# Two staging tiles, builds in fp32, and projections that stage values and split keys in a ring of five

## The chip, the cores and the metric

The kernel runs on one core of a Trainium2 chip. The metric is the device time of one execution in microseconds. TensorE is the engine of the matmuls, VectorE (DVE in the rows), ScalarE (ACT) and GpSimd (POOL) work on SBUF tiles, and SyncE (SP) issues nearly all plain transfers, in order; GpSimd issues the indirect ones.

## The reference, cut to what matters

One layer for two requests, 1024 prompt tokens and 64 sample tokens with 512 tokens of cache:

```python
h = rmsnorm(x)
zq, zk, zv, zcq, zckv, zkr, zg = split(h @ w_in)
o_a = differential_attention(zq, zk, zv)       # 8 heads, chunk-causal, relative bias
o_b = latent_attention(zcq, zckv, zkr)         # 16 heads, compressed keys and values
x = x + (sig(zg0) * (o_a @ w_a) + sig(zg1) * (o_b @ w_b)) @ w_out
h2 = rmsnorm(x)                                # expert part ("PEER"):
idx, g = two_stage_top16(h2 @ w_q, keys)       # 8 heads x 16 experts of 16384 per token
act = gelu(einsum("td,thkd->thk", h2, u[idx])) # 128 rows of u per token
x = x + einsum("thk,thkd->td", g * act, v[idx])
y = rmsnorm(x)
```

Outputs are y, the new keys and values and the new latents. All is fp32.

## The kernel before, in words

The 1088 tokens are nine tiles of 128 rows (the ninth has the 64 sample rows). Three groups of three tiles (`GROUPS`) go one after the other through projections, both attentions, output projection and expert scores. Group 0 splits its operands into two parts and uses three matmuls for one; groups 1 and 2 use plain fp32 matmuls. Then two passes over all of `peer_v` (`PASSES`: tiles 0 to 2, then 3 to 6) multiply a dense 128 x 16384 matrix of expert weights per tile with `peer_v`, in 16 chunks of 8 x 128 experts.

Beside this runs the expert part as background jobs, written as generators that `pump` advances while the main work is emitted: `route_job` (top-16, on VectorE), `dots_job`, `build_job`, and for tiles 8 and 7, which have no dense matrix, `vgather_job`. The job of a tile in a group's place runs in the next group; those of the last group run in the passes. The order that the chip gets is not quite the order of emission: a planner orders each engine's instructions with its own costs and the tiles' dependences, so a change of a tile's size or ring gives a new order everywhere. Each engine works through its list in order.

- **Dots (lines 338 to 365).** For each of the 128 experts of a row, `gather` (327) fetches one row of `peer_u` per token, 512 KB for a tile, with an indirect transfer from GpSimd into a buffer, and VectorE multiplies and sums it in place against h2 (line 358). There are four buffers `gb`, and in groups 1 and 2 three more, `gm`, in a pool `more` that opens when group 0 has given back its memory; three gathers of seven use `gm`. In the passes only `gb` exists. `vgather_job` uses the same `gather` on `peer_v` (line 453).
- **Builds (lines 367 to 426).** The dense matrix of a tile comes from its 128 indices and weights per token. The pair of indices of all experts of a token becomes two one-hot matrices, `oh1` and `oh2` (lines 402 and 403, 8 tokens at a time, a "step"; 16 steps per tile, 7 tiles, 112 steps). `oh2` is scaled by the weight, and a matmul over the 128 experts gives the token's 128 x 128 block. To keep fp32 weights in bf16 matmuls the weight is split into three bf16 parts (`a3`): three scaled copies `w3` (line 408 on ScalarE for part 0, eight instructions; line 411 on VectorE for parts 1 and 2) and three matmuls per token (line 418). ScalarE copies the result to `stage` (line 424), an 8 KB-per-partition tile that exists once; two steps fill it and one store writes it to `Ad` in memory. Of tile 6 (`TR`) the first `RC` = 9 chunks go into the resident tile `Ares` instead (line 422), and only the others to `Ad`; the passes load the rest as `araw`.
- **Projections.** `tmajor` makes 128 x 256 blocks. Keys go to `kt` (line 700, ring "P" of `PB` = 5 tiles), are transposed and split into `khl` (in the two-deep ring "Q") and stored to `kTd`. Values go through `vt` (line 720, the two-deep ring `z1`, which others use as well) and are stored to the output block by block.

Of the kernel before, what the change touches and what calls it, by code (L numbers as in the profile page):

```python
# [10 lines left out]
F32 = mybir.dt.float32  # L11
F32R = mybir.dt.float32r
BF16 = mybir.dt.bfloat16
I32 = mybir.dt.int32
U32 = mybir.dt.uint32
AF = mybir.ActivationFunctionType
ALU = mybir.AluOpType
# [3 lines left out]
D = 1024  # L21
# [16 lines left out]
GN = 384  # L38
# [2 lines left out]
NGB = 4  # L41
PB = 5
NB = 8
RC = 9
NWHOLE = 8
TR = 6
RATE_R2 = 0.41
# [12 lines left out]
def hybrid_tile(ctx: ExitStack, tc: tile.TileContext, A):  # L60
    nc = tc.nc
    V, S, G, PE, SP = nc.vector, nc.scalar, nc.gpsimd, nc.tensor, nc.sync

    def ld(out, in_):
        if out.dtype == F32R:
            out = out.bitcast(F32)
        if in_.dtype == F32R:
            in_ = in_.bitcast(F32)
        return SP.dma_start(out, in_)
# [34 lines left out]
    bp = ctx.enter_context(tc.tile_pool(name="bp", bufs=1))  # L104
# [10 lines left out]
    gturn = [0]  # L115
# [7 lines left out]
    def ptile(name, shape=(128, 1024), dt=F32):  # L123
        return att.tile(list(shape), dt, name=name, tag="P", bufs=PB)
# [10 lines left out]
    def z1(name):  # L135
        return sm.tile([128, 256], F32, name=name, tag="z1", bufs=2)
# [4 lines left out]
    def out_rows(name, t):  # L141
        return A[name + "_p"][t * 128:(t + 1) * 128] if t < 8 else A[name + "_s"]
# [183 lines left out]

    def gather(src, idx):
        gturn[0] += 1
        if cur["more"] and gturn[0] % 7 % 2:
            gb = cur["more"].tile([128, D], F32, name="gm", tag="gm")  # L330
        else:
            gb = cur["gp"].tile([128, D], F32, name="gb", tag="gb")
        G.indirect_dma_start(out=gb, out_offset=None, in_=src, in_offset=bass.IndirectOffsetOnAxis(ap=idx, axis=0))  # L333
        return gb
# [32 lines left out]
    def build_job(t):  # L367
        if t == TR:
            drain("r")
        src = bp.tile([128, 3, 128], F32, name="bsrc", tag="oh1")  # L370
        ld(src[:, 0, :], wgtd[t])
        ld(src[:, 1:3, :], efd[t])
        p = cur["ps"].tile([128, 512], F32, name="mm")
        pv = p.rearrange("p (a n) -> p a n", n=128)
        for i in range(3):
            PE.transpose(pv[:, i, :], src[:, i, :], ident)
        ixT = bp.tile([128, 2, 128], BF16, name="ixT")
        S.copy(ixT, pv[:, 1:3, :])
        aT = bp.tile([128, 128], F32, name="aT")
        S.copy(aT, pv[:, 0, :])  # L380
        a3 = bp.tile([128, 3, 128], BF16, name="a3")
        a3f = bp.tile([128, 128], F32, name="a3f")
        for i in range(3):
            V.tensor_copy(a3[:, i], aT)
            if i == 0:
                V.tensor_copy(a3f, a3[:, 0])
            if i < 2:
                V.tensor_tensor(aT, aT, a3[:, i], op=ALU.subtract)
        yield
        shp = [128, 4, 128, 2]  # L390
        iv = iota2[:, None, :, :].to_broadcast(shp)

        def over(row, tt):
            return row[:, tt:tt + 8].rearrange("p (g x) -> p g x", x=2)[:, :, None, :].to_broadcast(shp)

        n = RC if t == TR else 0
        for t0 in range(0, 128, 16):
            stage = bp.tile([128, 16, 4, 8, 4], F32, name="stage", tag="stage")
            for tt in range(t0, t0 + 16, 8):
                oh1 = bp.tile(shp, BF16, name="oh1", tag="oh1")  # L400
                oh2 = bp.tile(shp, BF16, name="oh2")
                V.tensor_tensor(oh1, iv, over(ixT[:, 1], tt), op=ALU.is_equal)  # L402
                V.tensor_tensor(oh2, iv, over(ixT[:, 0], tt), op=ALU.is_equal)  # L403
                w3 = bp.tile([128, 3] + shp[1:], BF16, name="w3")
                for i in range(3):
                    if i == 0:
                        for x in range(8):
                            S.activation(w3[:, 0, x // 2, :, x % 2], oh2[:, x // 2, :, x % 2], AF.Copy,  # L408
                                         scale=a3f[:, tt + x:tt + x + 1])
                    else:  # L410
                        V.tensor_tensor(w3[:, i], oh2, over(a3[:, i], tt), op=ALU.mult)
                for q in range(2):
                    p = cur["ps"].tile([128, 512], F32, name="mm")
                    pv = p.rearrange("p (a n) -> p a n", n=128)
                    for j in range(4):
                        x = 4 * q + j
                        for i in range(3):
                            PE.matmul(pv[:, j, :], lhsT=oh1[:, x // 2, :, x % 2], rhs=w3[:, i, x // 2, :, x % 2],  # L418
                                      start=i == 0, stop=i == 2)
                    pc = p.rearrange("p (t c i) -> p c i t", t=4, i=8)  # L420
                    if n:
                        S.copy(cur["Ares"][:, :, (tt + 4 * q) // 4], pc[:, :n])
                    if n < 16:
                        S.copy(stage[:, n:, (tt - t0) // 4 + q], pc[:, n:])
                    yield
            ld(Ad[t, :, n:, t0 // 4:t0 // 4 + 4], stage[:, n:])
# [149 lines left out]
    for g, tiles in enumerate(GROUPS):  # L576
# [117 lines left out]
        for j in range(4):  # L694
            w = wchunk(A["w_in"][2 + j])
            kt = ptile("kt", (128, 3, 256))
            for ti, t in enumerate(tiles):
                nr = tr(t)
                p = tmajor(hT, w, t)
                S.copy(kt[:nr, ti], p[:nr, :256])  # L700
                ld(out_rows("k", t)[:, j * 256:(j + 1) * 256], kt[:nr, ti])
            for hh in range(2):
                khl = att.tile([128, 2, GN], F32R, name="khl", tag="Q")
                pt = tpt()
                for ti, t in enumerate(tiles):
                    nr, l = tr(t), loc[t]
                    PE.transpose(pt[:, l:l + nr], kt[:nr, ti, hh * 128:hh * 128 + 128], ident[:nr, :nr])
                split(pt[:, :NH], khl[:, 0, :NH], khl[:, 1, :NH])
                dst = kTd[2 * j + hh]
                for i in range(2):  # L710
                    for l, tok, n in runs:
                        ld(bass.AP(tensor=dst.tensor, offset=dst.offset + 64 * i * T + tok,
                                   ap=[[(64 if i else 192) * T, 2], [T, 64], [1, n]]), khl[:, i, l:l + n])
        for j in range(4):
            w = wchunk(A["w_in"][6 + j])
            for t in tiles:
                nr = tr(t)
                p = tmajor(hT, w, t)
                vt = z1("vt")
                S.copy(vt[:nr], p[:nr, :256])  # L720
                ld(out_rows("v", t)[:, j * 256:(j + 1) * 256], vt[:nr])
        for j in range(8):
            w = wchunk(A["w_in"][14 + j])
            for hh in range(2):
# [613 lines left out]
```

## Time and profile before

| | |
|---|---|
| three runs | 4512.42, 4510.65, 4497.69 us; median 4510.65 |
| the profiled execution | 4499.18 us, its span 4497.4 us |
| TensorE, VectorE, ScalarE, GpSimd busy | 86%, 71%, 36%, 43% of the span |
| granted TensorE clock, mean | 0.892 of full speed |
| bytes moved | 1183 MB, 263 GB/s; 671 MB of it by the gathers |

The span counts from the first to the last instruction. Busy shares are means over stretches with different limits, so each stretch is read by itself. In a table of stretches the columns are the stretch, its length, the busy time of each engine (with its number of instructions), the granted clock of TensorE, the share of time that the DMA engines were in use, and GB/s. A row of waits says which engine sat idle before which instruction, and what ended that idle time.

### The profile page before, as it was taken

The numbers are of one execution on the slowest core, as the hardware profiler recorded it, in microseconds if no ns is written. First come the engines' busy times: TensorE is split into PE (matmuls) and PEld (weight loads), VectorE is DVE, ScalarE is ACT, GpSimd is POOL, SyncE is SP. The second block draws the span as 40 slices with busy tenths as digits, with TensorE's granted clock in tenths as the row PEclk, the third lists the DMA queues.
The fourth block names the chain that finished last, engine by engine and source line by source line (L and its number), as shares of the span: only waits on it lengthen the run. The fifth ranks groups of instructions, "written<-read, shape, count | busy, mean of one in ns | idle before, by whom it ended". The sixth has DMA issues, their size and how long they took to land.

```text
span 4497.4 us, 55226 instructions
## 1 busy us (share of the span) xinstructions
PE 3847.6 (86%) x18633; PEld 2898.2 (64%) x18633; DVE 3203.9 (71%) x7136; ACT 1603.3 (36%) x3656; POOL 1942.8 (43%) x1353
## 2 busy tenths in 40 slices
PE   6998988898788798887868877889999969999991
PEld 6977887556565565655546666654457858888881
DVE  4043457977788767797786777659847987777776
ACT  3344622025455513322454455133113532232320
POOL 3412241554456441143444656513434445545455
PEclk9967999987898898998778888989999979999995
DMA  5421244996777785697776767988868999989987
GB/s 176 168 96 56 67 170 169 352 350 231 267 263 269 272 320 216 226 329 290 245 248 239 256 239 253 351 291 311 320 246 317 349 328 332 351 312 352 321 314 260
DMA packets 467587, 1183.10 MB, mean 263 GB/s; under 512 B 45352, under 2 KB 218888, under 8 KB 452584
## 3 DMA queue, kind: packets, MB, share of 16 engines
q0 software_dynamic: 184320, 671.17, 41.4%
q1 hardware_dynamic: 282984, 508.41, 32.3%
q8 instruction: 147, 2.41, 0.2%
q14 instruction: 136, 1.11, 0.1%
HBM read 1074.60 MB, written 104.56 MB: 262 GB/s over the span
## 4 chain that ended last, share of the span: by engine, by line
PE 42%; DMA 13%; DVE 13%; issue 5%; ACT 4%; POOL 2%; SPq 0%; another core or an unknown queue 0%; ACTq 0%; POOLq 0%; DVEq 0%
PE acc_ps L1221 16%; PE mm L167 9%; PE acc_ps L1206 5%; DMA Ad<-stage 4%; DMA gb<-in_peer_v,beidx 3%; DVE gb L358 3%; DMA gb<-in_peer_u,beidx 2%; PE mm L418 2%; DVE gm L358 2%; POOL gb L333 2%; PE mm L827 2%; PE sc L795 1%; PE mm L952 1%; PE sc L793 1%; ACT w L408 1%
## 5 line engine op out<-in xcount | busy, mean ns | idle before, releaser
L333 POOL DMA_INDIRECT gb<-in_peer_u,beidx x758 | 1028.2, 1356 | 1364.7 <-DVE gb L358 811.1
L358 DVE SCALAR_TENSOR_TENSOR gb<-gb,h2r 128x1024 f32<-128x1024 f32 x758 | 918.3, 1220 | 174.4 <-DMA gb<-in_peer_u,beidx 157.9
L333 POOL DMA_INDIRECT gm<-in_peer_u,beidx x330 | 429.9, 1303 | 501.4 <-DVE gm L358 274.6
L1221 PE MATMUL acc_ps<-vhi,ahi 128*128 128x512 f32 x1408 | 439.9, 395 | 23.4 <-ACT ahi L1214 23.4
L1221 PE MATMUL acc_ps<-vhi,alo 128*128 128x512 f32 x1408 | 444.1, 396 | 3.0 <-DVE alo L1215 3.0
L1221 PE MATMUL acc_ps<-vlo,ahi 128*128 128x512 f32 x1408 | 441.0, 395 | 0.0
L358 DVE SCALAR_TENSOR_TENSOR gm<-gm,h2r 128x1024 f32<-128x1024 f32 x330 | 402.1, 1218 | 24.0 <-DMA gm<-in_peer_u,beidx 21.4
L333 POOL DMA_INDIRECT gb<-in_peer_v,beidx x192 | 268.0, 1396 | 229.7 <-DVE gacc L453 150.1
L167 PE MATMUL mm<-h,wraw 128*128 128x384 f32 (+1 forms) x1024 | 325.5, 479 | 20.4 <-ACT qd L739 10.4
L1206 PE MATMUL acc_ps<-vw,aw 128*128 128x512 f32 x768 | 335.0, 596 | 1.4 <-ACT aw L1202 1.4
L418 PE MATMUL mm<-w,oh 128*128 128x128 bf16 x2688 | 231.0, 237 | 111.5 <-DVE oh L402 50.5
L1221 PEld LDWEIGHTS acc_ps<-vhi,ahi 128*128 128x128 f32 x1408 | 265.6, 189 | 85.5 <-ACT ahi L1214 23.6
L453 DVE SCALAR_TENSOR_TENSOR gacc<-gb,vwgt,gacc 128x1024 f32<-128x1024 f32 x192 | 246.2, 1282 | 93.3 <-DMA gb<-in_peer_v,beidx 88.1
L1221 PEld LDWEIGHTS acc_ps<-vhi,alo 128*128 128x128 f32 x1408 | 265.0, 189 | 63.9 <-DVE alo L1215 3.7
L1221 PEld LDWEIGHTS acc_ps<-vlo,ahi 128*128 128x128 f32 x1408 | 265.5, 189 | 60.2 <-DVE vlo L1192 0.2
L408 ACT ACTIVATE w<-oh,a3f 128x128 bf16<-128x128 bf16 x896 | 280.8, 429 | 54.0 <-DVE oh L403 24.3
L179 POOL TENSOR_TENSOR wlo<-wraw,whi 128x2048 fp32r<-128x2048 f32 (+1 forms) x42 | 186.8, 4447 | 260.6 <-ACT whi L178 255.0
L418 PEld LDWEIGHTS <-oh 128*128 128x128 bf16 x2688 | 191.9, 106 | 160.6 <-issue 73.2
L167 PEld LDWEIGHTS mm<-h,wraw 128*128 128x128 f32 x1024 | 201.0, 199 | 133.8 <-issue 11.4
L167 PE MATMUL mm<-wraw,h 128*128 128x256 f32 (+1 forms) x960 | 235.6, 402 | 37.7 <-ACT vt L720 27.8
L1206 PEld LDWEIGHTS acc_ps<-vw,aw 128*128 128x128 f32 x768 | 145.5, 191 | 179.1 <-issue 175.6
L1214 ACT CAST ahi<-araw 128x1024 fp32r<-128x1024 f32 x79 | 82.8, 1049 | 474.4 <-PE acc_ps L1221 395.7
(384 smaller groups left out, 7574.2 us busy)
## 6 DMA issues: line engine op xcount, KB each, us to landing
vraw<-in_peer_v SPq DMA_DIRECT2D x192, 512.0 KB
wraw<-in_w_in SPq DMA_DIRECT2D x66, 1024.0 KB
araw<-Ad SPq DMA_DIRECT2D x103, 512.0 KB
Ad<-stage SPq DMA_DIRECT2D x48, 1024.0 KB
vw<-in_peer_v SPq DMA_DIRECT2D x64, 512.0 KB
wraw<-in_w_a SPq DMA_DIRECT2D x12, 1024.0 KB
wraw<-in_w_b SPq DMA_DIRECT2D x12, 1024.0 KB
wraw<-in_w_out SPq DMA_DIRECT2D x12, 1024.0 KB
```

What stands on the lines that cost most here:

```text
L167: PE.matmul(out, lhsT=L[0], rhs=R[0], start=start, stop=stop)
L179: G.tensor_tensor(lo[:, :n], raw[:, :n], hi[:, :n].bitcast(F32), op=ALU.subtract)
L333: G.indirect_dma_start(out=gb, out_offset=None, in_=src, in_offset=bass.IndirectOffsetOnAxis(ap=idx, axis=0))
L358: behind(V.scalar_tensor_tensor(gb, gb, 1.0, h2, op0=ALU.mult, op1=ALU.mult, accum_out=act[:, k:k + 1]))
L408: S.activation(w3[:, 0, x // 2, :, x % 2], oh2[:, x // 2, :, x % 2], AF.Copy, scale=a3f[:, tt + x:tt + x + 1])
L418: PE.matmul(pv[:, j, :], lhsT=oh1[:, x // 2, :, x % 2], rhs=w3[:, i, x // 2, :, x % 2], start=i == 0, stop=i == 2)
L453: behind(V.scalar_tensor_tensor(acc, gb, wgt[:, k:k + 1], acc, op0=ALU.mult, op1=ALU.add))
L793: PE.matmul(ps[:nq, a:b], lhsT=Q[:, c, qc:qc + nq], rhs=K[:, c, a - o:b - o], start=True, stop=False)
L827: PE.matmul(po[:nq, :128], lhsT=PT[:kw, b, :nq], rhs=Vt[:kw, b, :], start=b == 0, stop=b == nb - 1)
L1206: PE.matmul(pst[t][:, ds], lhsT=rv[:, i, :], rhs=vb[i][:, ds], start=c == 0 and i == 0, stop=False)
L1214: S.copy(av, rv)
L1221: PE.matmul(pst[t][:, ds], lhsT=L[:, i, :], rhs=R[:, ds], start=c == (0 if ip else NWHOLE and -1) and i == 0 and L is ahi and R is vb[i][0 ...
```

## The change

- `stage` becomes two tiles: the even ones stay in the pool `bp`, the odd ones come from the pool `more` in groups 1 and 2 and from `p2` in the passes.
- To make room, `gm` has one buffer instead of three, used by one gather of five, and `RC` is 7 instead of 9.
- A build's step has no split: `oh1` is copied to fp32 (`of`, ScalarE), `oh2` is multiplied by the fp32 weight (`w`, VectorE), and there is one fp32 matmul per token. `a3`, `a3f` and `w3` go.
- `khl` and `vt` are taken from the ring "P"; one `vt` holds the blocks of the group's three tiles.

```diff
-RC = 9
+RC = 7
...
-        if cur["more"] and gturn[0] % 7 % 2:
-            gb = cur["more"].tile([128, D], F32, name="gm", tag="gm")
+        if cur["more"] and gturn[0] % 5 == 1:
+            gb = cur["more"].tile([128, D], F32, name="gm", tag="gm", bufs=1)
...
-        a3 = bp.tile([128, 3, 128], BF16, name="a3")
-        a3f = bp.tile([128, 128], F32, name="a3f")
-        for i in range(3):
-            V.tensor_copy(a3[:, i], aT)
-            if i == 0:
-                V.tensor_copy(a3f, a3[:, 0])
-            if i < 2:
-                V.tensor_tensor(aT, aT, a3[:, i], op=ALU.subtract)
...
-            stage = bp.tile([128, 16, 4, 8, 4], F32, name="stage", tag="stage")
+            sp = (cur["more"] or cur["p2"]) if t0 % 32 else bp
+            stage = sp.tile([128, 16, 4, 8, 4], F32, name="stage", tag="stage", bufs=1)
...
-                w3 = bp.tile([128, 3] + shp[1:], BF16, name="w3")
-                for i in range(3):
-                    if i == 0:
-                        for x in range(8):
-                            S.activation(w3[:, 0, x // 2, :, x % 2], oh2[:, x // 2, :, x % 2], AF.Copy,
-                                         scale=a3f[:, tt + x:tt + x + 1])
-                    else:
-                        V.tensor_tensor(w3[:, i], oh2, over(a3[:, i], tt), op=ALU.mult)
+                of = bp.tile(shp, F32, name="of")
+                S.copy(of, oh1)
+                w = bp.tile(shp, F32, name="w")
+                V.tensor_tensor(w, oh2, over(aT, tt), op=ALU.mult)
...
-                        for i in range(3):
-                            PE.matmul(pv[:, j, :], lhsT=oh1[:, x // 2, :, x % 2], rhs=w3[:, i, x // 2, :, x % 2],
-                                      start=i == 0, stop=i == 2)
+                        PE.matmul(pv[:, j, :], lhsT=of[:, x // 2, :, x % 2], rhs=w[:, x // 2, :, x % 2],
+                                  start=True, stop=True)
...
-                khl = att.tile([128, 2, GN], F32R, name="khl", tag="Q")
+                khl = ptile("khl", (128, 2, GN), F32R)
...
-            for t in tiles:
+            vt = ptile("vt", (128, 3, 256))
+            for ti, t in enumerate(tiles):
                 nr = tr(t)
                 p = tmajor(hT, w, t)
-                vt = z1("vt")
-                S.copy(vt[:nr], p[:nr, :256])
-                ld(out_rows("v", t)[:, j * 256:(j + 1) * 256], vt[:nr])
+                S.copy(vt[:nr, ti], p[:nr, :256])
+                ld(out_rows("v", t)[:, j * 256:(j + 1) * 256], vt[:nr, ti])
```

## Rows read from the trace of the kernel before

**Rows 1.** The table of stretches: groups 1 and 2, attention, long pass, tail.

```profile
700.00:2975.00 2275.00, 1864.19 (x9375) 1360.30 (x9375) 1749.33 (x4235) 866.43 (x2267) 1024.46 (x768) 0.86 0.77 272
2045.00:2365.00 320.00, 231.41 (x1043) 156.97 (x1042) 243.99 (x453) 146.66 (x379) 126.03 (x92) 0.77 0.73 251
2420.00:2820.00 400.00, 324.44 (x2106) 259.35 (x2106) 304.08 (x512) 204.30 (x543) 233.75 (x151) 0.85 0.71 240
3690.00:4400.00 710.00, 709.46 (x3063) 575.95 (x3061) 552.29 (x610) 193.29 (x188) 386.90 (x274) 1.00 0.90 330
4400.00:4497.00 97.00, 0.00 (x0) 0.00 (x0) 66.44 (x103) 4.59 (x8) 49.20 (x39) 0.52 0.75 255
```

**Rows 2.** The chain that ended last, shares of the span by line (last one cut).

```profile
by line: PE acc_ps L1221 16.2%; PE mm L167 9.3%; issue 5.4%; PE acc_ps L1206 4.7%; DMA Ad<-stage 3.7%; DMA gb<-in_peer_v,beidx 3.3%; DVE gb L358 3.2%; DMA gb<-in_peer_u,beidx 2.1%; PE mm L418 2.0%; DVE gm L358 1.9%; POOL gb L333 1.7%; PE mm
```

**Rows 3.** Pieces of that chain: start us, us, what.

```profile
1143.91 11.28 DMA Ad<-stage
...
1336.58 6.60 DMA gm<-in_peer_u,beidx
...
1797.92 8.21 DMA Ad<-stage
...
1824.70 6.30 DMA Ad<-stage
...
2188.56 3.33 PE mm L827 x16
...
2726.68 12.52 DMA Ad<-stage
...
2836.74 19.43 DMA gm<-in_peer_u,beidx
```

**Rows 4.** Waits from 700 to 2975 us: total us, times, longest.

```profile
ACT stage L424 <- DMA Ad<-stage: 130.2, 28, 15.4
...
DVE gb L358 <- DMA gb<-in_peer_u,beidx: 40.0, 33, 3.6
...
PE mm L418 <- DVE oh L402: 37.1, 14, 6.0
PE mm L167 <- ACT stage L424: 36.3, 15, 7.7
...
DVE gm L358 <- DMA gm<-in_peer_u,beidx: 21.4, 24, 2.7
...
PE mm L418 <- ACT stage L424: 20.9, 6, 7.6
```

**Rows 5.** Groups of instructions: names, shapes, count | busy us, mean ns | idle before.

```profile
L408 ACT ACTIVATE w<-oh,a3f 128x128 bf16<-128x128 bf16 x896 | 280.8, 429 | 54.0 <-DVE oh L403 24.3 <-DVE a3f L386 15.8 <-PE mm L418 10.8
...
L1202 ACT COPY aw<-araw 128x1024 f32<-128x1024 f32 x24 | 25.0, 1042 | 123.7 <-PE acc_ps L1206 105.6 <-issue 15.6 <-DMA araw<-Ad 2.0
...
L411 DVE TENSOR_TENSOR w<-oh,a 128x1024 bf16<-128x1024 bf16 x224 | 145.3, 684 | 0.1
...
L1215 DVE TENSOR_TENSOR alo<-araw,ahi 128x1024 fp32r<-128x1024 f32 x79 | 96.5, 1222 | 79.5 <-ACT ahi L1214 78.5 <-DMA vraw<-in_peer_v 0.8
...
L418 PE MATMUL mm<-w,oh 128*128 128x128 bf16 x2688 | 231.0, 237 | 111.5 <-DVE oh L402 50.5 <-ACT stage L424 20.9 <-DVE w L411 17.0
```

**Rows 6.** Pieces of the chain between 2440 and 2560 us.

```profile
2499.65 0.69 PE mm L418 x12
```

**Rows 7.** Who waited for the values' tile: us, times.

```profile
  PE mm L167: 27.8, 7
...
  PE mm L153: 9.2, 2
```

**Rows 8.** Stretches of the dots alone (line 358), then VectorE's waits, 3690 to 4400.

```profile
700.00:2975.00 2275.00, 913.96 (x1536) 0.86 0.77 272
...
DVE gacc L453 <- DMA gb<-in_peer_v,beidx: 63.5, 53, 2.9
DVE gb L358 <- DMA gb<-in_peer_u,beidx: 51.6, 41, 3.3
```

## The prediction

> **What bounds the kernel now.** I read the table of stretches first [rows 1]. The span falls into three parts: group 0 (0 to 700 us, no builds and no dots), groups 1 and 2 (700 to 2975, where dots, builds and routing are mixed into the projections and the attention), and the passes with their tail (2975 to 4497). In the long pass (3690 to 4400) the reader is to see TensorE at 709 of 710 us and a granted clock of 1.00: nothing that this change touches in the groups can shorten that. In two attention stretches of group 2 TensorE is busy 231 of 320 us and 324 of 400, at a granted clock of 0.77 and 0.85, a mean over its two levels of 1.2 and 2.4 GHz: there it waits for others, and part of its work runs at the lower level. The tail (4400 to 4497) has no matmul at all; it is the last value gathers. So the time that can move is the idle time inside groups 1 and 2: 2275 - 1864 = 411 us [rows 1].
>
> Next the chain that ended last [rows 2]: 3.7% of it, 166 us, is the landing of the store of a build's staging tile. All of that lies in groups 1 and 2, in 15 long pieces of 6 to 18 us, of which the first and the last stand in [rows 3]. Then the waits of these groups [rows 4]: ScalarE sat 130.2 us in 28 waits, up to 15.4 us, before it could copy a finished build into the one staging tile, because that tile's store had not landed. ScalarE is in order, so the copies that free the projections' accumulators stand behind it: TensorE waited 36.3 us for that at the projections and 20.9 us at the builds' own matmuls.
>
> **The second staging tile.** Two steps of a build fill a tile and two more may now fill the other while the first is stored. In the longest wait ScalarE was held 15.4 us [rows 4]; two steps take some 27 us (two landings in a row begin at 1797.9 and 1824.7 [rows 3]), so nearly every landing is covered and the 130 us on ScalarE go. What it is worth: at least the 57 us that TensorE waited directly (36.3 + 20.9), at most the 130 us of ScalarE, as the chain's 166 us holds waits that other work would fill. What is late next is VectorE's order of dots and reductions, which the chain also runs through. I take -85, nearer to the TensorE rows. SP issues the same stores at the same points; its queue gets no new entry here.
>
> **The builds in fp32: ScalarE.** Eight scaled copies per step take 280.8/112 = 2.51 us of ScalarE [rows 5]; in their place comes one copy of 128x1024, which takes 1.04 us by the nearest row (L1202, also to fp32). That is 1.47 x 112 = 165 us less ScalarE. It is off TensorE's path mostly; what waits behind are exponentials and transposed probabilities of the attention. Bounds: 0 and -45 (about 1% of the chain is this line). I take -15.
>
> **VectorE.** Two bf16 products of 0.684 us become one fp32 product; 128x1024 fp32 with two inputs takes 1.22 us (L1215) [rows 5]. 1.37 - 1.22 = 0.15 us x 112 = 17 us less busy time. The operand tiles stay single, so the copy and the product wait for the step's matmuls before; ScalarE's staging copies of that step, ahead of it in the queue, wait for the same matmuls today, so nothing new stands behind. Of more weight is the order: today the next step's first one-hot tile is the matmuls' own operand, so it can't be written until they end, and TensorE then waited 37.1 us for it [rows 4]. In the changed build the matmuls read copies, so the one-hots of the next step are made while they run, and only the product and one copy come behind. Bounds 0 and -50; I take -15.
>
> **TensorE.** 12 bf16 matmuls go in 0.69 us [rows 6], so a step's 24 in 1.38 us. 128-column fp32 matmuls go 16 in 3.33 us [rows 3], 0.208 each, so a step's 8 take 1.66 us. +0.28 x 112 = +32 us, 9 of it in the passes, where TensorE is the bound and all counts, 23 in the groups, where I count half: +20. Bounds: -40 (if a step's true cost is nearer the 231/112 = 2.06 us that the line is busy per step, [rows 5]) and +185, if fp32 operands with a stride of two elements, of which the trace has none, ran at half the pace; the bf16 operands have that stride now and lose nothing by it (0.69/12 = 57 ns for 128 columns), so I stay near the lower end.
>
> **Values and split keys in the ring of five.** TensorE waited 27.8 and 9.2 us for the copy of the values into the two-deep ring, which waits for stores to land [rows 7]; for the split keys' tiles I count nothing. The ring of five is taken by one key tile and two split tiles per block of columns, so a slot comes back after five allocations in place of two; with one tile of values for three blocks of rows, the fifth has long landed. The same stores go through SP, one per block as before. Bounds 0 and -37; I take -33. No tile of the attention is delayed, since its first probabilities come after the gates, which turn the ring over three times.
>
> **Five gather buffers in place of seven.** This is the price. Each dot on VectorE needs a gathered row block, and POOL can issue the gather only when its buffer's last dot is done. In groups 1 and 2, with seven, 768 dots (1536 instructions, two each) [rows 8] cost VectorE 40.0 + 21.4 = 61 us of waiting for landings [rows 4], 0.08 us each. In the long pass, where four serve today and will, the 274 gathers [rows 1] cost 63.5 + 51.6 = 115 us [rows 8], 0.42 each. So the price lies between nothing and 0.34 x 768 = 261 us on VectorE. Landings that the chain shows are 6.6 us at the easy end and 19.4 at the worst [rows 3]; dots come every 2275/768 = 3.0 us on the mean and take 1.2, so five buffers give a gather some 5 x 3.0 - 1.2 = 13 us and cover the common landing, but dots come in bunches. I take 0.2 us per dot, 0.12 more than now: 92 us on VectorE, of which half reaches the end, since TensorE has matmuls of other units queued: +45.
>
> The Trainium skill, "DMA: Bandwidth & Descriptors", section "Anatomy of one DMA — SWDGE (gpsimd) path", gives about 2.0 us plus bytes over 436 GB/s, an estimate of 3.2 us for one gather of 512 KB. By that five buffers would cost nothing and this term would be 0. The chain's landings of 6.6 to 19.4 us [rows 3] differ from it, under the load of the other transfers, and the row decides.
>
> **Fewer resident chunks.** Two more chunks of the one resident tile come back from memory in the long pass (512 KB each; at its 330 GB/s [rows 1] 1.6 us each) and its build stores 9/16 instead of 7/16: +3 at most, as that pass has its loads ahead. Its matmuls and copies stay the same in number.
>
> **Sum.** -85 - 15 - 15 + 20 - 33 + 45 + 3 = -80. The profiled execution's own time is 4499 us (span 4497.4), 11 below the median of the runs shown, 4511. 4499 - 80 = 4419 for one execution like the profiled one; I give 4420 and hold the 11 us as spread. The passes, from 2975 on, are carried over as they are: their gathers keep four buffers, and their end stays some 97 us behind the last matmul [rows 1].
>
> **Rivals.**
>
> *Much faster.* The whole chain share of the staging tile goes (-130), the one-hot loop gives its -50, ScalarE's freed time -30, the values -33, and five buffers cost next to nothing because landings of 7 us fit into five intervals of dots (+10); with TensorE +20 and +3: -210, so 4290; halfway to it is 4350. For it: the granted clock of 0.77 and 0.85 in the attention stretches [rows 1] would rise with fewer holes, which I haven't counted. Against it: in those stretches the chain also runs through dots. Chance 0.22.
>
> *No change.* ScalarE's wait was covered after all: when the store is no longer late, VectorE's dots are, and half of TensorE's 57 us comes back (-28), with the values (-33); dots (+45), fp32 matmuls (+20) and chunks (+3) take it: +7, so 4506. For it: ScalarE waited 130 us for the store and TensorE only 57 for ScalarE [rows 4], so more than half was covered. Against: the chain's 3.7%. Chance 0.12 (4470 to 4520).
>
> *Slower: starved dots.* One mechanism: POOL issues too late with five buffers, and VectorE, in order, holds the reductions and products that the attention's exponentials wait for. At the long pass's 0.42 us per dot VectorE loses 261 us; with two thirds on the path +174, against the lower gains (-57 - 33 + 20 + 3 = -67): +107, so 4606. Against the other terms of the sum (-125) it decides from 125 us reaching the end, 188 on VectorE, 0.32 us per dot. For it: POOL idles for buffers now, with seven; the bunches. Against: the long pass has four buffers and the DMA engines 0.90 of their time in use, the attention stretches 0.73 and 0.71 [rows 1]. Chance 0.14.
>
> *The change doesn't take.* The planner, whose order of every engine is made anew from its own costs, may put the builds' steps elsewhere, so that the second staging tile is never used while the first is stored; then the fp32 builds and the values remain: about 4499 - 15 - 33 + 20 + 45 = 4516. Chance 0.04.
>
> **How the numbers follow.** Forecast (4380 to 4470) 0.48, much faster 0.22, no change 0.12, slower 0.14, not taken 0.04. Likeliest 4420. The range leaves one tenth at either side: 4325 to 4520. Against the median of 4511, 0.3% is 14 us, about what a measurement of this kernel can tell from no change (its runs lie 15 us apart): faster than 4497 by forecast, much faster and half of no change, 0.76; within, half of no change and half of not taken, 0.08; slower 0.16.
>
> **What would show it.** In the changed profile ScalarE's wait for the staging store should fall from 130 us to under 20, and that share of the chain from 3.7% to under 1%; the copy that replaces the scaled ones should take about 1.05 us and the product 1.22; the step's eight matmuls 1.7 us at full clock. ScalarE should be busy some 165 us less. VectorE's waits for gathered rows before 2975 us should rise from 61 to about 150 us. The passes should begin 80 us earlier than at 2975 and keep their length. The forecast is wrong if the groups are as long as before although the staging wait is gone, if the matmuls of fp32 with stride two take 3 us a step, or if VectorE's waits for gathers rise by more than 200 us.

## The result and the profile after

The changed kernel takes 4440.41 us at the median (4434.02 to 4451.86), the kernel before 4507.77 us beside it: 0.9856 of before, with an interval of 0.9829 to 0.9883. Measured again later it gave 0.9860 (0.9836 to 0.9885); below I use the mean of the two, 0.9858, which is 64 us less than before (the medians of the first measure lie 67 apart). 80 were forecast. The forecast of 4420 was right in its sign, in its main cause and within its range, and 20 us too low; that its sum came so near is in part luck, as the part on the prediction tells.

The profiled execution after has a span of 4450.1 us, 47 less than the one before; it is the slowest of the four after, and the one before was 9 us faster than the median there. I read the stretches first, as in [rows 1] (us; TensorE, its weight loads, VectorE, ScalarE and GpSimd busy with the counts of instructions; granted clock, DMA share, GB/s).

```profile
700.00:2920.00 2220.00, 1859.96 (x8688) 1382.55 (x8687) 1735.30 (x4098) 758.35 (x1698) 995.95 (x768) 0.86 0.80 278
...
3640.00:4348.00 708.00, 708.00 (x3061) 575.22 (x3060) 549.18 (x610) 193.21 (x188) 399.99 (x272) 1.00 0.91 331
4349.00:4449.00 100.00, 0.00 (x0) 0.00 (x0) 69.86 (x105) 4.60 (x8) 51.20 (x41) 0.51 0.76 258
```

Groups 1 and 2 take 2220 us in place of 2275, and TensorE idles 360 of them in place of 411: 51 of the 55 us are idle time, and its busy time is nearly the same (1860 and 1864), though the builds now take more of it. The long pass and the tail are as they were. Where the 47 us lie is seen from where each stage begins (keys and queries by their first copy on ScalarE, the others by their first matmul):

| stage begins at, us | before | after | gained or lost in the stage before it |
|---|---|---|---|
| keys, group 1 | 714.6 | 706.3 | -8 |
| queries | 935.4 | 942.0 | +15 (projections) |
| first output projection | 1189.7 | 1209.9 | +14 (differential attention) |
| second output projection | 1585.5 | 1571.8 | -34 (latent attention) |
| keys, group 2 | 1801.1 | 1782.2 | -5 |
| queries | 2039.9 | 1988.8 | -32 (projections) |
| first output projection | 2365.3 | 2324.8 | +11 (differential attention) |
| second output projection | 2819.0 | 2764.5 | -14 (latent attention) |
| pass 0 | 2990.1 | 2934.8 | -1 |
| end | 4497.4 | 4450.1 | +10 in pass 0, -2 in all the rest |

Next the chain that ended last, by line, which answers to [rows 2]:

```profile
by line: PE acc_ps L1209 19.6%; issue 6.1%; PE acc_ps L1194 4.6%; PE mm L167 2.4%; POOL gb L333 2.2%; DMA gb<-in_peer_v,beidx 1.8%; DMA gb<-in_peer_u,beidx 1.7%; DVE gb L358 1.3%; PE mm L406 1.2%; PE mm L815 1.0%; PE sc L783 0.8%; PE sc L78
```

The landing of the staging tile's store, 3.7% of the chain before, is gone from it. Of the waits in the groups (total us, times, longest), beside [rows 4]:

```profile
ACT stage L412 <- PE mm L406: 254.0, 124, 9.7
...
DVE gb L358 <- DMA gb<-in_peer_u,beidx: 101.4, 83, 4.6
...
ACT rB L548 <- DVE rB L547: 81.4, 3, 38.3
...
PE mm L406 <- DVE w L400: 49.0, 17, 7.9
...
PE mm L167 <- ACT gt L715: 44.6, 3, 27.9
...
DVE gm L358 <- DMA gm<-in_peer_u,beidx: 28.2, 22, 6.0
```

No line has ScalarE waiting for a staging store any more (130.2 us before). ScalarE waits for the builds' matmuls instead, which is the right order. Four waits are new or longer: VectorE's for gathered rows (101.4 + 28.2 = 129.6 us; 61.4 before), TensorE's for the builds' fp32 product (49.0 us), TensorE's for the gates' copies (44.6 us), which had almost none, and ScalarE's for what a route's exponential reads (81.4 us; 37.4 before). The groups of the builds' instructions, beside [rows 5] (names, shapes, count, busy us, mean ns, idle before):

```profile
L406 PE MATMUL mm<-w,of 128*128 128x128 f32 x1792 | 284.0, 310 | 71.5 <-DVE w L400 58.9 <-ACT of L398 6.8 <-DVE sf L806 2.1
...
L400 DVE TENSOR_TENSOR w<-oh,aT 128x1024 f32<-128x1024 bf16 x112 | 136.5, 1219 | 48.6 <-PE mm L406 46.6 <-issue 1.6
L398 ACT CAST of<-oh 128x1024 f32<-128x1024 bf16 x112 | 117.7, 1051 | 14.9 <-DVE oh L395 14.7
```

The copy takes 1.05 us and the product 1.22, as forecast. TensorE's line has 1792 records for 896 matmuls: the profile shows an fp32 matmul as two. A whole step in the passes, where the granted clock is 1.00, is this piece of the chain, beside [rows 6]; the second piece is a step at the lower clock:

```profile
3094.92 1.88 PE mm L406 x16
...
2755.68 3.75 PE mm L406 x16
```

### The profile page after: what moved, and what is told of

Read it like the earlier page. It is cut to its first block, busy times and chain, and to the rows that moved or that the text cites. A ratio compares the mean times of both kernels' runs of the same rounds, so it can differ in the third digit from the quotient of the medians.

```text
span 4450.1 us, 52506 instructions
## 1 busy us (share of the span) xinstructions
PE 3858.4 (87%) x17737; PEld 2944.7 (66%) x17737; DVE 3188.8 (72%) x6982; ACT 1454.8 (33%) x2874; POOL 1931.8 (43%) x1353
## 4 chain that ended last, share of the span: by engine, by line
PE 32%; DMA 6%; issue 6%; DVE 5%; POOL 3%; ACT 1%; SPq 0%; POOLq 0%; DVEq 0%; ACTq 0%
PE acc_ps L1209 20%; PE acc_ps L1194 5%; PE mm L167 2%; POOL gb L333 2%; DMA gb<-in_peer_v,beidx 2%; DMA gb<-in_peer_u,beidx 2%; DVE gb L358 1%; PE mm L406 1%; PE mm L815 1%; PE sc L783 1%; PE sc L781 1%; DMA wgtd<-act 1%; DMA gm<-in_peer_u,beidx 0%; POOL gm L333 0%; DMA vw<-in_peer_v 0%
## 5 line engine op out<-in xcount | busy, mean ns | idle before, releaser
L333 POOL DMA_INDIRECT gb<-in_peer_u,beidx x934 | 1233.1, 1320 | 1540.1 <-DVE gb L358 940.9
L358 DVE SCALAR_TENSOR_TENSOR gb<-gb,h2r 128x1024 f32<-128x1024 f32 x934 | 1127.6, 1220 | 232.3 <-DMA gb<-in_peer_u,beidx 211.9
L333 POOL DMA_INDIRECT gb<-in_peer_v,beidx x192 | 280.5, 1461 | 220.0 <-DVE gacc L441 133.1
L167 PE MATMUL mm<-h,wraw 128*128 128x384 f32 (+1 forms) x1024 | 322.7, 475 | 51.7 <-ACT gt L715 44.6
L406 PE MATMUL mm<-w,of 128*128 128x128 f32 x1792 | 284.0, 310 | 71.5 <-DVE w L400 58.9
L333 POOL DMA_INDIRECT gm<-in_peer_u,beidx x154 | 201.5, 1308 | 307.7 <-DVE gm L358 114.8
L406 PEld LDWEIGHTS mm<-w,of 128*128 128x128 f32 x1792 | 265.0, 222 | 99.7 <-issue 61.6
L412 ACT COPY stage<-mm 128x512 f32<-128x512 f32 (+1 forms) x224 | 125.2, 560 | 381.8 <-PE mm L406 346.8
L1178 ACT CAST vhi<-vraw 128x1024 fp32r<-128x1024 f32 x192 | 201.0, 1052 | 103.8 <-DMA vraw<-in_peer_v 50.3
L167 PE MATMUL mm<-wraw,h 128*128 128x256 f32 (+1 forms) x960 | 224.4, 389 | 8.5 <-ACT vt L708 6.0
```

The source lines that it names most:

```text
L167: PE.matmul(out, lhsT=L[0], rhs=R[0], start=start, stop=stop)
L358: behind(V.scalar_tensor_tensor(gb, gb, 1.0, h2, op0=ALU.mult, op1=ALU.mult, accum_out=act[:, k:k + 1]))
L406: PE.matmul(pv[:, j, :], lhsT=of[:, x // 2, :, x % 2], rhs=w[:, x // 2, :, x % 2], start=True, stop=True)
L1178: S.copy(hi, raw)
```

## The experiments

**The four parts alone, on the kernel before.** Theory: the second staging tile makes the gain and pays for it with gathers. Rival: the fp32 builds make it, by 150 us less on ScalarE (1603 to 1455 us busy); or the ring does.

```diff
 five buffers:    -if cur["more"] and gturn[0] % 7 % 2:    +if cur["more"] and gturn[0] % 5 == 1:   (gm: bufs=1)
 fp32 builds:     -w3 in three bf16 parts, 24 matmuls      +of, w in fp32, 8 matmuls
 ring:            -khl in "Q", vt = z1("vt")               +khl, vt = ptile(...)
 second tile:     +sp = (cur["more"] or cur["p2"]) if t0 % 32 else bp    (with five buffers and RC = 7)
```

> The kernel before, with five gather buffers in groups 1 and 2 in place of seven and nothing else (the 8 KB that this frees stay empty). Theory (the gain of the change is the second staging tile, and the lost gather buffers take a part of it back): VectorE's waits for gathered rows before 2975 us rise from 61 us to about 130 us, as in the changed kernel (129.6), and about half of the 68 us reaches the end: +20 to +50 us. Rival A (five buffers cost nothing, since a landing fits into five intervals of dots): within 14 us of before. Rival B (the price of the long pass, 0.42 us per dot): +100 us or more.

Measured: 1.0028 of before (1.0012 to 1.0045), +13 us. VectorE's waits in the groups rose just as in the changed kernel (total us, times, longest):

```profile
DVE gb L358 <- DMA gb<-in_peer_u,beidx: 89.8, 72, 4.9
...
DVE gm L358 <- DMA gm<-in_peer_u,beidx: 31.3, 24, 5.8
```

121.1 us in place of 61.4, and only 13 of these 60 us reach the end: a fifth, not the half that I counted. So the waits came as the theory had them, and by the ratio the time as rival A did (within 14 us).

> The kernel before, with the fp32 builds and nothing else (one staging tile, seven gather buffers, nine resident chunks, the old rings). Theory: ScalarE is busy some 150 us less, but still waits for the staging tile's store, 130 us or more before 2975 us; TensorE's builds take 53 us more, of which 10 lie in pass 0 and all count; the first one-hot tile no longer holds TensorE (37 us). Together -30 to +10 us. Rival (the fp32 builds are the source of the gain, since ScalarE was the engine that TensorE waited for): -40 us or more.

Measured: 1.0033 (1.0015 to 1.0052), +15 us: the rival falls, and the theory's +10 was too low. The waits show where ScalarE's freed time went:

```profile
ACT stage L411 <- DMA Ad<-stage: 184.0, 22, 16.9
...
PE mm L167 <- ACT stage L411: 54.9, 13, 12.0
```

ScalarE waits 184.0 us for the same store (130.2 before), and TensorE behind it 54.9 (36.3 before). While a landing bounds the step, faster work in front of it only waits longer.

> The kernel before, with the values and the split keys in the ring of five and nothing else. Theory: TensorE's 37 us of waiting for the values' tile go, and a part comes back at the gates of group 1, which sit in the same ring behind stores that wait on SP (in the changed kernel TensorE waits 45 us there): -25 to 0 us. Rival A (the prediction's own price, nothing given back): -33 us. Rival B (the ring is the source of the gain): -45 us or more.

Measured: 1.0051 (1.0034 to 1.0067), +23 us, outside what the theory and both rivals gave. TensorE's wait for the values fell from 27.8 to 12.8 us, but at the gates of group 1 a new and longer one stood:

```profile
PE mm L167 <- ACT gt L727: 50.9, 2, 26.1
...
ACT rB L560 <- DVE rB L559: 32.6, 2, 29.4
```

> The kernel before, with the second staging tile and what makes room for it (five gather buffers, seven resident chunks); builds in bf16 parts and the old rings stay. Theory: ScalarE's 130 us of waiting for the staging store fall under 20 us; -85 for it and +45 for the gathers, with +3 for the chunks: -60 to -25 us. Rival A (the fp32 builds are the source; the stall on ScalarE was covered): within 14 us, or slower. Rival B (the whole of the chain's share comes back, 166 us, and the gathers cost nothing): -80 us or more.

Measured: 0.9853 (0.9824 to 0.9882), -71 us by medians (4435.71 beside 4506.24): the whole gain of the change, from this part alone, more than the theory's -60 and less than rival B's -80. ScalarE's waits for the staging store are gone from its trace, and TensorE's for the staging copies at the projections fell from 36.3 to 6.1 us. Against five buffers alone the second tile is 0.9853/1.0028 = 0.9826, or -79 us; I had taken -85.

**Parts taken back from the changed kernel.**

```diff
 one tile:    -stage = sp.tile(...)               +stage = bp.tile(...)
 bf16:        -of, w in fp32, 8 matmuls           +w3 in three bf16 parts, 24 matmuls
 old rings:   -khl, vt = ptile(...)               +khl in "Q", vt = z1("vt")
```

> The changed kernel with one staging tile again (fp32 builds, the ring of five, five gather buffers and seven resident chunks stay). Singly, on the kernel before, five buffers cost +13 us (0.28% of 4506), fp32 builds +15, the ring +23, and the second tile with five buffers gave -66 to -71. Theory (the second tile carries the whole gain): all three costs without it, 4506 + 13 + 15 + 23 = 4557 us, some 115 us above the changed kernel (1.024 to 1.028 of it, 1.008 to 1.014 of before). Rival (together, the fp32 builds and the ring give something that they don't give singly, as the changed kernel is only as fast as the second tile alone in spite of their 38 us): at or under 4520 us, within 0.3% of before.

Measured: 1.0015 (1.0001 to 1.0030), under the theory's 1.008 and within the rival's 0.3% of before. Without the second tile nothing of the gain is left, and its worth in the changed kernel is 0.9858/1.0015 = 0.984, -71 us. The three costs did not add, though: their product is 1.0112. So the single prices of 0.3 to 0.5% hold in their own surroundings only. The planner orders every engine anew for each kernel; how much of these prices is that order stays open.

> The changed kernel with the builds in three bf16 parts again, so the second tile, five buffers, seven chunks and the ring of five. Theory A (the single prices add): 4436 + 23 = 4459 us. Theory B (the ring's 23 us were paid because stores of the staging tile and the ring's stores held ScalarE together, and go with the second tile): 4436 to 4445 us. Rival (the fp32 builds give back what the ring costs, by 150 us less on ScalarE): above 4460.

Measured: 0.9811 (0.9789 to 0.9832), the fastest version here, under what either theory gave. The ring is now worth 0.9811/0.9853 = 0.996, and the fp32 builds on top of it cost 0.9858/0.9811 = 1.005, some 20 us. The two medians are of different chips, so I compare them by their ratios only.

> The changed kernel with the values and split keys in their old rings, so the second tile, five buffers, seven chunks and the fp32 builds. Theory A (the single prices add): 4436 + 15 = 4451 us. Theory B (with the second tile ScalarE's 150 us are worth something): 4415 to 4436 us, as fast as or faster than the second tile alone. Rival (the ring is worth its 33 us in this surrounding): 4460 us or more, slower than the changed kernel by over 0.4%.

Measured: 0.9853 (0.9830 to 0.9876), between theory A and B: the fp32 builds cost nothing beside the old rings, and the ring then gives nothing (0.9858/0.9853).

One cost of the fp32 builds is the same everywhere: pass 0, from its first matmul to its last, takes 647.2 to 654.1 us in the nine kernels here with bf16 builds (649.7 on the mean, 649.8 in the kernel before) and 658.8 to 663.0 in the five runs with fp32 builds (660.4; 660.2 in the changed kernel). That is 11 us, 0.2%.

**Staging in half tiles.** Two tiles of 8 tokens fit where one of 16 was, so that all seven gather buffers stay.

```diff
-for t0 in range(0, 128, 16):
-    stage = bp.tile([128, 16, 4, 8, 4], F32, name="stage", tag="stage")
+for t0 in range(0, 128, 8):
+    stage = bp.tile([128, 16, 2, 8, 4], F32, name="stage", tag="sh%d" % (t0 // 8 % 2), bufs=1)
...
```

> The kernel before, with its one staging tile of 16 tokens cut in two of 8 that take turns, one step of a build each: no memory more, so seven gather buffers and nine resident chunks stay. The stores are twice as many and their contiguous runs half as long (256 bytes in place of 512). Theory A (what counts is that ScalarE can copy into one tile while the other is stored): the gain of the second tile without the price of the gathers, -84 us, so 4415 to 4430 us. Theory B (a tile now comes back after one step, some 13 us, and the landings are 6 to 18 us, so a part of ScalarE's wait stays, and the short runs lengthen the landings): 4440 to 4480 us, with 30 us or more of ScalarE waiting for the store. Rival (the short runs load the DMA engines so that dots and weights are late): at or above 4506 us.

Measured: 0.9854 (0.9834 to 0.9874), the time of theory B and as good as the second whole tile, with gathers at 48.3 us and 19.2 us of waiting for the store, less than theory B's 30. A price that the whole tiles don't pay is seen in the DMA queue of the plain transfers (packets, MB, share of 16 engines' span; the kernel before first):

```profile
q1 hardware_dynamic: 282984, 508.41, 32.3%
```

```profile
q1 hardware_dynamic: 389352, 508.41, 33.6%
```

The same 508.41 MB take 0.336 x 4465 = 1500 us of all engines in place of 0.323 x 4497 = 1453. The Trainium skill, "DMA: Bandwidth & Descriptors", section "Specifications", asks for at least 512 bytes for line rate; the trace agrees in direction, with 47 us more of engine time for runs of 256. Over all the kernels here this queue's transfers take 1437 to 1460 us in the twelve with runs of 512, and 1500 and 1510 us in the two with runs of 256.

```diff
+i3 = t0 // 8 % 3
+sp = bp if i3 < 2 else (cur["more"] or cur["p2"])      (gm: every third gather, bufs=2; RC = 8; the ring of five)
+stage = sp.tile([128, 16, 2, 8, 4], F32, name="stage", tag="sh%d" % i3, bufs=1)
...
```

> The kernel before with three staging tiles of 8 tokens in turn, six gather buffers, eight resident chunks and the ring of five (bf16 builds): 12 KB of staging in place of the changed kernel's 16. Theory (two half tiles left 19 us of waiting for the store and gathers at 48 us; a third one takes that store wait away, and six buffers keep the gathers near 85 us): 0.975 to 0.981 of before, some 5 to 25 us under the second whole tile with the ring (0.9811). Rival (stores twice as many, with runs of 256 bytes, cost as much as the gathers give): 0.981 to 0.986.

Measured: 0.9908 (0.9890 to 0.9927), slower than both theories had it. The store's wait is gone and the gathers wait 62.6 us, so it isn't these; it has the same load on the queue (391544 packets, 33.8%) and the gates' wait of 48.6 us. Why it loses 0.5% against two half tiles isn't settled.

**The changed kernel again, and the gates.** In every kernel with the ring of five up to here TensorE waits 30 to 51 us for the gates' copies of group 1, about as much as the ring takes away at the values. Two kernels ask what makes this wait and what it is worth; both start from the bf16 version of the changed kernel.

> The changed kernel itself once more, beside the two below, to have it at the same precision (its first measure was 0.9856 of before, 0.9829 to 0.9883). Theory (the fp32 builds cost some 10 to 20 us net, mostly through TensorE's 53 us more): 0.984 to 0.987, so above the same kernel with bf16 builds, which gave 0.9811 (0.9789 to 0.9832). Rival (that difference was spread between runs, the fp32 builds cost nothing here): 0.981 to 0.983.

Measured: 0.9860 (0.9836 to 0.9885): the theory; bf16 builds with the ring are better by some 0.5%, with intervals that just don't touch.

```diff
-ld(gateT[g, 2 * j + hh, :, :NH], gt[:, :NH])
+(S.dma_start if g == 1 else ld)(gateT[g, 2 * j + hh, :, :NH], gt[:, :NH])
```

> The changed kernel with bf16 builds, and the gates' stores of group 1 issued from ScalarE in place of SP, so that they no longer stand behind the route's stores. In that kernel TensorE waits 45 us for the gates' copies there (47.0 by its weight loads), ScalarE 30 us for the store of a gate, and SP up to 38 us behind a gate and 26 behind the route's tile. Theory (SP's order holds the gates): these waits fall under 15 us and the time by 15 to 40 us, to 4395 to 4420 where that kernel has 4434. Rival (VectorE's route work bounds this stretch, and ScalarE waits 44 us for it in order anyway, with the gates behind): within 10 us of that kernel, with TensorE's wait for the gates at 35 us or more.

Measured: 0.9831 (0.9811 to 0.9851): no gain, as the rival had it. SP is out of it, and the wait stayed, with another name:

```profile
ACT rB L561 <- DVE rB L560: 50.5, 2, 43.8
...
PE mm L167 <- ACT gt L728: 35.9, 2, 35.3
```

ScalarE stands 43.8 us at the exponential of a route, whose operand VectorE hasn't made yet; two gates stand behind it in its list. Why the operand comes late is seen in the dots that VectorE has to do in front of it. These are the instructions of line 358 from the second of the routes' exponentials in group 1 to the third, this one (the second tile alone, then with the ring):

```profile
828.10:912.10 84.00, 39.33 (x65) 1.00 0.94 351
```

```profile
829.90:933.50 103.60, 57.56 (x94) 0.81 0.90 323
```

In the six kernels here with the old rings there are 62 to 69 of them, two for each dot, and the third exponential starts at 912 to 922 us; in the seven with the ring of five and this rate of routes there are 88 to 94, and it starts at 930 to 938. So the order that the ring brought puts some 13 dots more in front of it, 18 us of VectorE in the pair shown. No run here changes these dots alone.

The last run takes the exponential out of the gates' way: fewer route steps are emitted in group 1, so that this exponential comes behind the last query copy.

```diff
-RATE_R_G = (0.7, 0.7, 0.623)
+RATE_R_G = (0.7, 0.5, 0.623)
```

> The changed kernel with bf16 builds (0.9811 of before, and 0.9831 with the gates' stores on ScalarE), and the rate at which group 1 emits route steps lowered from 0.7 to 0.5, nothing else. By that ScalarE's list has the third exponential of the routes behind the last query copy in place of behind the 14th gate. In the kernel with the gates' stores on ScalarE, ScalarE stood 45 us at that exponential (892 to 937 us) with two gates behind it, and TensorE 35 us. Theory (this exponential, not SP and not the ring, is what gave the ring's gain back): TensorE's wait for the gates' copies falls from 45 us to under 15, and the time by 15 to 40 us, to 0.973 to 0.978 of before. Rival (VectorE's route bounds the stretch: the attention of group 1, whose reductions stand behind the route on VectorE, starts no earlier): the wait moves to the queries or the first scores, and the time stays within 0.979 to 0.985 of before.

Measured: 0.9886 (0.9857 to 0.9915): the wait went, as the theory said, and the time didn't fall. It lies above the rival's range too (0.979 to 0.985), and the rival's reason fails with it, since the attention did start earlier. TensorE's wait for the gates in this stretch fell from 45.2 to 8.3 us, and the first scores came at 918.9 us in place of 958.9. But the stretch of the attention behind (same columns as the first view; the bf16 kernel, then this one):

```profile
803.00:945.00 142.00, 96.82 (x279) 55.70 (x278) 124.78 (x428) 15.05 (x24) 71.81 (x59) 0.83 0.91 330
945.00:1250.00 305.00, 251.75 (x1113) 172.38 (x1112) 234.88 (x422) 139.70 (x371) 138.64 (x108) 0.80 0.76 266
```

```profile
803.00:945.00 142.00, 126.89 (x383) 73.42 (x382) 134.09 (x489) 22.63 (x43) 62.61 (x57) 0.95 0.94 342
945.00:1250.00 305.00, 224.51 (x966) 156.74 (x966) 229.21 (x423) 125.35 (x336) 139.12 (x110) 0.73 0.75 257
```

TensorE gets 30 us more done up to 945 us and 27 us less from there to 1250, at a granted clock of 0.73 in place of 0.80. The first output projection begins 15 us earlier (1208.7 to 1193.6), the latent attention 8 (1262.6 to 1254.9), the second output projection 3 later (1569.7 to 1572.6). The 40 us were lent, not won. TensorE's waits from 945 to 1250 us show where most of them went (the bf16 kernel, then this one):

```profile
PE mm L828 <- DMA Vt<-out_v_p: 9.6, 3, 4.7
```

```profile
PE mm L828 <- DMA Vt<-out_v_p: 25.4, 4, 9.8
...
PE sc L794 <- DMA K<-kTd: 9.1, 1, 9.1
```

It waits 34.5 us in place of 9.6 for the values and keys that the attention loads back from memory. Its waits for VectorE grew less, from 22 to 27 us, and VectorE is busy 229 of these 305 us (235 in the bf16 kernel), so VectorE as the bound, the rival's reason, isn't shown here. Why these loads land late wasn't tested, and why the median is even 0.7% above the bf16 kernel's isn't seen in this profiled execution.

## Why the prediction was right, and where it was not

**The second staging tile** (-85): right, by two pairs of kernels: -79 (over five buffers alone) and -71 (over the changed kernel with one tile), each uncertain by 10 to 15 us, since two intervals combine. The place was right too: -34 and -14 us in the latent attentions and -32 in group 2's projections, where 97 of the 130 us of ScalarE's store waits were (43, 23 and 31).

**The fp32 builds** (-15 on ScalarE, -15 on VectorE, +20 on TensorE): wrong in sign. Measured +15, 0 and +22 us in three surroundings, against -10 together. The copy and the product took what I said, and ScalarE is 149 us less busy (165 forecast); none of that reached the end: with one staging tile TensorE didn't wait for ScalarE's work but for the landing behind it, and with two it waits for the staging copies at the projections for 6.1 us only, so little was left to win. VectorE's term fell because the wait only changed its name: TensorE waited 37.1 us for a one-hot tile and 12.7 for the product, and waits 49.0 for the product now, since that tile is single and is written only when the step's matmuls are done. TensorE's term was mis-sized: a step takes 1.88 us at full clock, not 1.66. I had taken 16 records of the row at 2188.56 [rows 3] for 16 fp32 matmuls; they are 8, and the engine was mostly at its lower clock there (granted 0.57 from 2188 to 2192 us). So the builds' line rose by 53 us (231.0 to 284.0), not 32, 10 of it in pass 0, where it all counts. The operands' stride of two costs nothing, as I had said: contiguous fp32 matmuls of the attention (line 815) run at nearly the same pace, 16 records in 1.80 us at a granted clock of 1.00.

```profile
2116.63 1.80 PE mm L815 x16
```

The Trainium skill, "FP8 and Floating Point Precision", section "TensorE Precision Notes", says that true fp32 takes four passes through the array. The trace agrees: 1.88/8 = 0.235 us is 4.1 times the 0.057 us of a bf16 matmul [rows 6], so 8 fp32 matmuls are 32 passes where three bf16 parts are 24.

**The values and split keys in the ring** (-33): the mechanism was there (TensorE's wait for the values fell from 27.8 to 6.0 us) and the sum was not: +23, -19 and +2 us in three surroundings, nothing on the mean; with the uncertainty of each, only the +23 is far from zero. The step that failed is "no tile of the attention is delayed": I had asked what the ring delays by its slots, and not what the new order of every engine delays. In group 1's projections ScalarE's list has a route's exponential in front of the last gates. With the ring TensorE comes earlier to the gates, the exponential comes later, behind some 13 more dots on VectorE, and TensorE waits there: these projections take 14 us more (223 to 237, second tile alone and with the ring). In group 2, where TensorE waits only 1 us for gates, the ring shortens them by 10 us (208 to 198). That the dots are the whole cause stays open: with the exponential out of the way the projections were 45 us shorter (237 to 192), and the kernel wasn't faster.

**Five gather buffers** (+45): VectorE's wait is as forecast (129.6 and 121.1 us, 150 forecast), 0.17 us per dot; the share that reaches the end is a fifth (13 of 60), not half. This error and the ring's cancel almost exactly, 32 us one way and 33 the other, and that is luck: it is why the sum came out near.

**Fewer resident chunks** (+3): not separable from the rest; the long pass takes 712.8 us in place of 716.8, so it costs nothing that shows.

**The passes** should have begun 80 us earlier and "keep their length". They begin 55 us earlier, and pass 0 doesn't keep its length (+10), for the fp32 matmuls, of which I had put 9 us there and then not in this sentence.

**The rivals.** "Starved dots" fell with the 0.17 us per dot, where it needed 0.32. "No change" fell with the second tile's -71 to -79. "Much faster" needed ScalarE's freed time and the one-hot loop to count, and they didn't; nor did the granted clock in the groups rise (0.86 before and after). "The change doesn't take" fell with ScalarE's store waits, which are gone.

By the measured prices, -75 + 12 + 0 + 13 = -50 us; the kernel gave -64. The difference is within what the pairs are uncertain by, and the single prices don't add here anyway.

## What to carry to other kernels

An engine that is stalled on a landing is mended by a second buffer, not by less work: of this change, which freed 149 us of one engine and changed the arithmetic of another, the buffer was the gain. A change of a tile's ring also moves work that has nothing to do with the tile, here dots on VectorE, so look at the order of each engine around a new wait. Before counting a removed wait as time, look at what the stretch behind it waits for: here 40 us won at the gates were gone again by the second output projection. Count fp32 matmuls by their records and at the clock of their row.

## What the runs showed of the hardware

An fp32 matmul of 128 columns is two records of 117 ns at the clock's upper level of 2.4 GHz and costs 4.1 bf16 ones. A step of 8 takes 1.88 us there, and 3.75 at the lower level of 1.2 GHz. Halving the contiguous run of a store from 512 to 256 bytes added 47 us of all DMA engines' time for the same bytes in one kernel (1453 to 1500), and the other kernel with such runs has 1510.
